# Routed feed-forward stage: blocks of two experts in turn, strips of 512 columns, whole 8 KB places

## The chip, the cores and the metric

The kernel runs on one core of a Trainium2 chip. The metric is device time in microseconds of one execution, with all weights read from HBM. The engines that matter are TensorE (PE, with its weight loads shown as PEld), VectorE (DVE), ScalarE (ACT), GpSimd (POOL) and SyncE (SP), which issues the weight transfers.

## What is computed

Two model blocks follow each other on 256 tokens of width 1024, in float32. The first block has two layers of token mixer and feed-forward; in its second layer the feed-forward is routed:

```python
logits = t @ router_w + router_b
top_v, top_i = lax.top_k(logits, 2)              # 2 of 8 experts for each token
gates = softmax(top_v)
combine = sum(one_hot(top_i, 8) * gates[..., None], axis=1)
for e in range(8):
    y_e = (silu(t @ w_gate[e]) * (t @ w_up[e])) @ w_down[e]   # 1024 -> 3584 -> 1024
    out = out + combine[:, e:e + 1] * y_e
```

The second block has two layers of feed-forward (2816 wide), latent attention with a convolution, and another feed-forward. Only the routed stage is rewritten by the change; elsewhere some buffers are allocated in other units.

## The kernel before

The stages run one after the other: `mix0, ffn0, mix1, moe, f1_0, mla0, f2_0, f1_1, mla1, f2_1`. The weights are laid out in HBM as units of 128 rows by 2048 float32 (1 MB, 8 KB in each partition), in the order in which they are used; `weight_plan` writes that order, and `Stream` loads unit after unit through SP's queue. A unit goes into a *place*. Four places (`RAW`) serve the whole program. In the routed stage more are lent: two from a pool of its own, six from the buffers of split weights (`hl`), and some from pools that lie idle then. `load()` issues the next transfer as soon as the queue of free places holds one. A transfer's issue on SP waits until the last reader of that place is done; `give` returns the places of a step at the step's end, and SP runs in program order.

In the routed stage (`moe`) each expert has 96 slots for tokens, in three groups of 32. `gather` brings the tokens of a pair of experts into `xe`. The work is cut into 56 steps, expert by expert, 7 blocks of 512 hidden columns each. A block takes four units for gate and up (woven: 128 columns of gate, 128 of up, and so on) and two for down.

- `gate_up` (L1076 to L1092): the 32 tokens of a group are the stationary operand, so that one matmul fills 32 of the 128 output partitions. Four matmuls that stand in four strips of the array run at once; each strip takes 256 columns of the unit. ACT takes SiLU of the gate half, DVE multiplies by the up half.
- `turn_g` (L1094 to L1102) transposes the product with matmuls of 32 columns against the identity.
- `down` (L1104 to L1128) multiplies by the down units, again 32 tokens stationary and four strips of 256 columns, and adds up in PSUM over the 7 blocks. After the last block the sums go to `yf`.
- `back` (L1130) splits `yf` in a high and a low part and scatters it to the tokens, scaled by the gate.

Groups 0 and 1 (`main`) are always computed, group 2 (`rest`) only when the expert has more than 64 tokens: its gate_up, turn and down stand in one `tc.If(counts[c] > 64)` at the end of the step (L1181). With 64 tokens or fewer every engine jumps over that code. In this text a *heavy* expert has more than 64 tokens and a *light* one has not. A second `If` (L1170), in step 15, holds the whole code for experts with more than 96 tokens (`second`); it does not run with these inputs. Before it every engine must still get past it. In step i the order on PE is gate_up of block i, down of block i-1, turn of block i, then the rest.

All fp32 matmuls that are not marked float32r show as two instructions in the trace, each with a weight load of its own.

Of the kernel before, what the change touches and what calls it, by code (L numbers as in the profile page):

```python
# [18 lines left out]
D = 1024  # L19
# [14 lines left out]
MORE = 2  # L34
STAGES = ("mix0", "ffn0", "mix1", "moe", "f1_0", "mla0", "f2_0", "f1_1", "mla1", "f2_1")


def blocks_of(f):
    return [(f0, min(512, f - f0)) for f0 in range(0, f, 512)]

# [30 lines left out]
def weight_plan(stages):  # L71
# [30 lines left out]
    def plan_moe():  # L102
        seq = [(e, b) for e in range(NE) for b in range(F1 // 512)]
# [162 lines left out]
def model(ctx, tc, A, out, stages=STAGES):  # L266
# [47 lines left out]
    turn = load_rows([("norm1_g", 16)], tp, "gl", nc.sync, 4)  # L314
# [95 lines left out]
    def xt():  # L410
        return [xp.tile([128, 8, 128], F32R, tag=n, name=n) for n in ("xh", "xl")]
# [89 lines left out]
    def ffn(key, f, nin, nout, half=None):  # L501
# [37 lines left out]
        def turn_g(b, tag="mm"):  # L539
            w = bl[b][1] // 128  # L540
            g = g32.pop(b)
            gh[b], gl[b] = [], []
            for t in range(2):
                ps = turn4([g[t][:, i * 128:(i + 1) * 128] for i in range(w)], tag)
                h = tp.tile([128, 4, 128], F32R, tag="gh", name="gh", bufs=4)
                l = tp.tile([128, 4, 128], F32R, tag="gl", name="gl", bufs=4)
                cut2(h[:, :w], l[:, :w], ps)
                gh[b].append(h)
                gl[b].append(l)
# [54 lines left out]
    def mixer1(l, nin, nout, c, pool):  # L604
# [27 lines left out]
        a_sb = []  # L632
        for t in range(2):
            a = tp.tile([128, 512], F32, tag="gl", name="az", bufs=4)
            nc.scalar.activation(a[:, :256], ps_a[t][:, :256], AF.Copy, scale=nin.r[t])
            a_sb.append(a)
        ps_g = project(("gx", l), 2, nin, 512, K2)
        z, zw = [], []
        for t in range(2):
            b = a_sb[t][:, 256:]  # L640
            nc.scalar.activation(b, ps_g[t][:, :256], AF.Copy, scale=nin.r[t])
            nc.vector.scalar_tensor_tensor(b, ps_g[t][:, 256:], nin.r[t], b, ALU.mult, ALU.mult)
            z.append(b)
            q = tp.tile([128, 2, 256], F32, tag="gl", name="zw", bufs=4)
# [15 lines left out]
        dT2 = tp.tile([128, 2, 256], F32, tag="gh", name="dT", bufs=4)  # L660
# [12 lines left out]
        for t in range(2):  # L673
            ac = tp.tile([128, 2, 256], F32, tag="gh", name="ac", bufs=4)
# [89 lines left out]
    def mla(l, nin, nout, c, pool):  # L764
# [68 lines left out]
        for nm, n, g in (("q", 3, "q_latent_norm_2"), ("k", 2, "kv_latent_norm_2")):  # L833
            for t in range(2):
                lh[nm, t], ll[nm, t] = (tp.tile([128, 4, 128], F32R, tag=i, name="lat", bufs=4)[:, :n] for i in ("gh", "gl"))
                cut2(lh[nm, t], ll[nm, t], turn4([lat[nm, t][0][:, i * 128:(i + 1) * 128] for i in range(n)]), gain(g, l))
# [95 lines left out]
        with tc.high_priority(offset=100):  # L932
            for t in range(2):
# [10 lines left out]
                s = tp.tile([128, 4, 128], F32, tag="gl", name="cs", bufs=4)  # L944
# [90 lines left out]
    def moe(R, nout, pool):  # L1035
# [3 lines left out]
        seq = [(e, b) for e in range(NE) for b in range(nb)]  # L1039
# [6 lines left out]
        def lent(p, names, w=D, **kw):  # L1046
            return lambda: [p.tile([128, w], F32, tag=n, name="raw", **kw) for n in names]
# [28 lines left out]

        def gate_up(i, gs):

            e, b = seq[i]
            if ("gu", i) not in held:  # L1080
                held["gu", i] = [W.hold(((("moe", e), "gu", b), j)) for j in range(4)]
            units = held["gu", i]
            ps, n = bank(), len(gs)
# [5 lines left out]
            s = prod[i, gs] = tp.tile([128, 512], F32, tag="g32", name="gs", bufs=4)[:, :n * 128].rearrange("p (g c) -> p g c", g=n)  # L1089
            v = ps[:, :n * 256].rearrange("p (g c) -> p g c", g=n)  # L1090
            nc.scalar.activation(s, v[:, :, 0:128], AF.Silu)  # L1091
            nc.vector.tensor_tensor(s, v[:, :, 128:256], s, op=ALU.mult)  # L1092

        def turn_g(i, gs):  # L1094

            s, n = prod.pop((i, gs)), len(gs)
            ps = bank()
            for g in range(n):
                for c in range(4):
                    nc.tensor.matmul(ps[32 * c:32 * c + 32, g * 128:(g + 1) * 128], s[:, g, 32 * c:32 * c + 32], ident, start=True, stop=True)  # L1100
            a = gT[i, gs] = pool.tile([128, n, 128], F32, tag=f"gT{gs[0]}", name="gT", bufs=2)
            nc.scalar.activation(a, ps[:, :n * 128].rearrange("p (g c) -> p g c", g=n), AF.Copy)  # L1102

        def down(i, gs):  # L1104
# [4 lines left out]
            for g in gs:  # L1109
                if b == 0:  # L1110
                    y[e, g] = bank("acc")
            a = gT.pop((i, gs))
            for j in range(4):
                for c, g in enumerate(gs):
                    for q in range(4):
                        nc.tensor.matmul(y[e, g][32 * q:32 * q + 32, :256], a[:, c, 32 * j:32 * j + 32], units[j // 2][0](j % 2, q * 256, 256),  # L1116
                                         start=b == 0 and j == 0, stop=b == nb - 1 and j == 3)
            if b == nb - 1:
                if e not in yf:
                    yf[e] = pool.tile([SLOTS, D], F32, tag="yf", name="yf", bufs=1)  # L1120
                    nc.gpsimd.memset(yf[e][64:SLOTS], 0.0)
                for g in gs:
                    for q in range(4):
                        o, a = yf[e][32 * g:32 * g + 32, q * 256:(q + 1) * 256], y[e, g][32 * q:32 * q + 32, :256]
                        if q % 2:
                            nc.vector.tensor_copy(o, a)
                        else:
                            nc.scalar.activation(o, a, AF.Copy)  # L1128
# [25 lines left out]
        for i in range(n + 1):  # L1154
            e, b = seq[i] if i < n else (NE, 0)
            now, before_ = [], []
            if i < n:
                gate_up(i, main)
                now += [lambda: gate_up(i, rest)]
            if i == 0:  # L1160
                _, counts = nc.values_load_multi_w_load_instructions(R.counts[0:1, :NE + 1], min_val=0, max_val=T,
                                                                            skip_runtime_bounds_check_because="the values are only compared")
# [6 lines left out]
            if (e, b) == (2, 1):  # L1169
                with tc.If(counts[NE] > SLOTS, preferred_fallthrough_block=False):  # L1170
                    for base in range(SLOTS, T, 128):
                        second(R, base)
            if i:
                down(i - 1, main)
                (now if b else before_).append(lambda: down(i - 1, rest))
            if i < n:
                turn_g(i, main)
                now += [lambda: turn_g(i, rest)]
            for c, fs in ((e - 1, before_), (e, now)):
                if fs:  # L1180
                    with tc.If(counts[c] > 64):  # L1181
                        for f in fs:
                            f()
            W.give(held.pop(("gu", i), []) + held.pop(("d", i - 1), []))
            if i and b == 0:
                back(e - 1)
# [81 lines left out]
    def post_of(ap):  # L1268
        t = xp.tile([128, D], F32, tag="xh", name="post")
# [69 lines left out]
```

## Time and profile before

| | |
|---|---|
| median of 3 runs | 2383.78 us (2382.59 to 2389.35) |
| the profiled execution's own time | 2385.31 us |
| its span, first to last instruction | 2382.9 us |
| mean granted TensorE clock | 0.976 |
| PE busy | 2253.9 us (95%) |
| DMA packets | 599.95 MB, mean 252 GB/s |

The span is what the profile covers; the execution's own time is 2.4 us longer. The time of a kernel on PE is not read from its busy share here: matmuls of one strip overlap with those of the others, so a stretch in which PE is busy can be one in which it waits a little after each instruction. What is read is the length of stretches, PE's idle time in them, and the granted clock.

### The profile page before, as it was taken

What the parts mean: (1) busy time and instruction counts of PE and PEld (TensorE: products, weight loads), DVE (VectorE), ACT (ScalarE), POOL (GpSimd) and SP (SyncE); (2) the same over time, 40 slices, a digit from 0 to 9 for tenths busy, and PEclk for the clock granted to TensorE, in tenths of its full rate; (3) what the DMA queues carried; (4) which work ended last, traced back from release to release, by engine and by line L of the source; (5) the groups of instructions that cost most, each with busy time, mean ns of one, the idle gap of its engine ahead of it and who ended that gap; (6) DMA issues with size and microseconds to landing.
All of it is one profiled execution on the core that took longest, in us unless ns stands there. A gap on an engine that the chain in (4) does not pass through costs nothing. (4 is left out here: it accounts for less than half of the span.)

```text
span 2382.9 us, 49084 instructions
## 1 busy us (share of the span) xinstructions
PE 2253.9 (95%) x21632; PEld 1746.0 (73%) x21632; DVE 929.2 (39%) x1262; ACT 795.0 (33%) x1259; POOL 171.2 (7%) x258
## 2 busy tenths in 40 slices
PE   8999999889989989988998899998999999989998
PEld 7888888556757656755675588886888888877887
DVE  5654564201010101010110354576645645587554
ACT  5544444101010101010110344465534544475443
POOL 3000012000000000000000100042000100050000
PEclk9999999899999999999999899999999999999999
DMA  7655554899979999999999655440555455432552
GB/s 270 222 190 185 187 210 179 323 379 402 366 289 403 382 406 390 399 392 396 382 395 389 224 210 182 167 177 21 201 180 190 177 189 182 148 130 94 198 179 87
DMA packets 112529, 599.95 MB, mean 252 GB/s; under 512 B 14652, under 2 KB 17118, under 8 KB 50204
## 3 DMA queue, kind: packets, MB, share of 16 engines
q1 hardware_dynamic: 111996, 595.82, 66.1%
q8 instruction: 195, 3.19, 0.5%
q10 hardware_dynamic: 288, 0.52, 0.1%
q14 instruction: 50, 0.41, 0.0%
HBM read 595.25 MB, written 1.05 MB: 250 GB/s over the span
## 5 line engine op out<-in xcount | busy, mean ns | idle before, releaser
L231 DVE TENSOR_TENSOR wl<-raw,wh 128x1024 fp32r<-128x1024 f32 (+2 forms) x456 | 540.7, 1216 | 430.9 <-ACT wh L230 430.5
L230 ACT ACTIVATE wh<-raw 128x1024 fp32r<-128x1024 f32 (+2 forms) x456 | 454.3, 1035 | 484.2 <-PE mm L391 302.3
L1087 PE MATMUL mm<-raw,xe 128*32 128x256 f32 x8960 | 535.9, 390 | 30.8 <-issue 26.9
L1087 PEld LDWEIGHTS mm<-raw,xe 128*32 128x32 f32 x8960 | 340.6, 113 | 192.8 <-issue 51.0
L388 PE MATMUL mm<-wh,xh 128*128 128x512 f32 (+3 forms) x1280 | 472.9, 372 | 3.1 <-ACT xh L407 3.1
L389 PE MATMUL mm<-wl,xh 128*128 128x512 f32 (+3 forms) x1280 | 471.3, 371 | 0.0
L391 PE MATMUL mm<-wh,xl 128*128 128x512 f32 (+3 forms) x1280 | 394.3, 371 | 0.3 <-DVE xl L408 0.3
L1092 DVE TENSOR_TENSOR gs<-mm,gs 128x256 f32<-128x256 f32 (+1 forms) x84 | 32.0, 380 | 741.5 <-ACT gs L1091 465.5
L1116 PE MATMUL acc<-raw,gT 128*32 128x256 f32 x4480 | 277.8, 386 | 16.4 <-PEq L1181 8.7
L388 PEld LDWEIGHTS mm<-wh,xh 128*128 128x128 f32 x1280 | 241.6, 189 | 44.0 <-ACT xh L407 3.5
L389 PEld LDWEIGHTS mm<-wl,xh 128*128 128x128 f32 x1280 | 241.8, 189 | 40.8 <-DVE wl L231 0.6
L391 PEld LDWEIGHTS mm<-wh,xl 128*128 128x128 f32 x1280 | 236.8, 189 | 41.0 <-DVE xl L408 1.0
L1116 PEld LDWEIGHTS acc<-raw,gT 128*32 128x32 f32 x4480 | 172.9, 112 | 97.3 <-issue 24.4
L1091 ACT ACTIVATE gs<-mm 128x256 f32<-128x256 f32 (+1 forms) x84 | 29.2, 348 | 598.9 <-PE mm L1087 598.9
L388 PE MATMUL acc<-wh,gh 128*128 128x512 f32 x464 | 186.0, 401 | 0.0
L389 PE MATMUL acc<-wl,gh 128*128 128x512 f32 x464 | 183.4, 395 | 0.0
L391 PE MATMUL acc<-wh,gl 128*128 128x512 f32 x464 | 145.3, 393 | 0.0
L371 POOL TENSOR_SCALAR s<-s 128x1 f32<-128x1 f32 (+1 forms) x60 | 32.3, 538 | 1171.2 <-ACT junk L378 1068.3
L391 PEld LDWEIGHTS acc<-wh,gl 128*128 128x128 f32 x464 | 87.3, 188 | 20.7
L389 PEld LDWEIGHTS acc<-wl,gh 128*128 128x128 f32 x464 | 87.6, 189 | 19.0
L388 PEld LDWEIGHTS acc<-wh,gh 128*128 128x128 f32 x464 | 87.5, 188 | 18.7
L1102 ACT ACTIVATE gT<-mm 128x256 f32<-128x256 f32 (+1 forms) x84 | 28.6, 348 | 186.4 <-PE mm L1100 186.1
(256 smaller groups left out, 1694.4 us busy)
## 6 DMA issues: line engine op xcount, KB each, us to landing
raw<-in_w_moe_dram SPq DMA_DIRECT2D x268, 1024.0 KB
raw<-in_w_f_dram SPq DMA_DIRECT2D x132, 1024.0 KB
raw<-in_w_moe_dram SPq DMA_DIRECT2D x184, 256.0 KB
raw<-in_w_ffn_dram SPq DMA_DIRECT2D x42, 1024.0 KB
raw<-in_w_mix_dram SPq DMA_DIRECT2D x23, 1024.0 KB
raw<-in_w_moe_dram SPq DMA_DIRECT2D x44, 512.0 KB
raw<-in_w_mla_dram SPq DMA_DIRECT2D x18, 1024.0 KB
raw<-in_w_mla_dram SPq DMA_DIRECT2D x8, 576.0 KB
```

The source lines that it names most:

```text
L230: self.nc.scalar.activation(h[:, s], t, AF.Copy)
L231: self.nc.vector.tensor_tensor(l[:, s], t, h[:, s].bitcast(F32), op=ALU.subtract)
L371: nc.gpsimd.tensor_scalar(r, ms, EPS, None, ALU.add)
L388: nc.tensor.matmul(o, sh[:, k, :], h[:, j, a:b], start=first and i == 0, stop=False)
L389: nc.tensor.matmul(o, sh[:, k, :], l[:, j, a:b], start=False, stop=False)
L391: nc.tensor.matmul(o, sl[:, k, :], h[:, i + (r[0] if r else 0), a:b], start=False, stop=last and i == n - 1)
L1087: nc.tensor.matmul(ps[32 * j:32 * j + 32, c * 256:(c + 1) * 256], xe[e // 2][:, k, e % 2, 32 * g:32 * g + 32], units[k // 2][0](k % 2, j * ...
L1091: nc.scalar.activation(s, v[:, :, 0:128], AF.Silu)
L1092: nc.vector.tensor_tensor(s, v[:, :, 128:256], s, op=ALU.mult)
L1102: nc.scalar.activation(a, ps[:, :n * 128].rearrange("p (g c) -> p g c", g=n), AF.Copy)
L1116: nc.tensor.matmul(y[e, g][32 * q:32 * q + 32, :256], a[:, c, 32 * j:32 * j + 32], units[j // 2][0](j % 2, q * 256, 256), start=b == 0 and ...
```

## The change

The order of the blocks comes from `moe_order`: block 0 of expert 0, block 0 of expert 1, block 1 of expert 0, and so on, pair by pair. The plan of the weights follows it. Down comes two steps after gate_up (`LAG = 2`), so that it belongs to the same expert as the block whose gate_up runs, except at the change of pairs. For two groups together the four strips are now (group 0, columns 0 to 511), (group 0, 512 to 1023), (group 1, ...), (group 1, ...): one matmul has 512 columns. The turn is one 128x128 transpose for each 128 columns. All places that are lent are now whole units: `xh` and `xl` are one tile `x`, and `gh` and `gl` of two token tiles are one tile `ghl` (the places out of `gn` and `t32` are gone). The `If` around `second` loses its argument on which side falls through.

```diff
+def moe_order():
+    return [(e, b) for p in range(0, NE, 2) for b in range(F1 // 512) for e in (p, p + 1)]
...
-            if i:
-                dn(*seq[i - 1])
-        dn(*seq[-1])
+            if i >= LAG:
+                dn(*seq[i - LAG])
+        for s in seq[-LAG:]:
+            dn(*s)
...
     def xt():
-        return [xp.tile([128, 8, 128], F32R, tag=n, name=n) for n in ("xh", "xl")]
+        x = xp.tile([128, 2, 8, 128], F32R, tag="x", name="xhl")
+        return [x[:, 0], x[:, 1]]
+
+    def quarters(dt, shape=(4, 128)):
+        a = tp.tile([128, 2, 2, *shape], dt, tag="ghl", name="ghl")
+        return [[a[:, i, t] for t in range(2)] for i in range(2)]
...
-        W.extend([(lent(hlp, (n,), UNIT), end - 6) for n in ("wh", "wl") * HL]
-                 + [(lent(xp, ("xh", "xl")), end - 16), (lent(xp, ("xh", "xl")), first + 30)]
-                 + [(lent(tp, ("gh", "gh", "gl", "gl"), 512, bufs=4), end - 16)] * 2
-                 + [(lent(tp, ("gn", "gn", "t32", "t32"), 512), first + 70)])
+        W.extend([(lent(hlp, n), end - 6) for n in ("wh", "wl") * HL] + [(lent(xp, "x"), end - 16), (lent(xp, "x"), first + 30 * LAG)]
+                 + [(lent(tp, "ghl"), end)] * 2)
...
+        def strips(gs):
+            return [(g, c) for g in gs for c in range(4 // len(gs))]
...
-            for c, g in enumerate(gs):
-                for k in range(8):
-                    for j in range(4):
-                        nc.tensor.matmul(ps[32 * j:32 * j + 32, c * 256:(c + 1) * 256], xe[e // 2][:, k, e % 2, 32 * g:32 * g + 32],
-                                         units[k // 2][0](k % 2, j * 256, 256), start=k == 0, stop=k == 7)
+            n = 256 * len(gs)
+            ps = bank()
+            for k in range(8):
+                for j, (g, c) in enumerate(strips(gs)):
+                    nc.tensor.matmul(ps[32 * j:32 * j + 32, :n], xe[e // 2][:, k, e % 2, 32 * g:32 * g + 32],
+                                     units[k // 2][0](k % 2, c * n, n), start=k == 0, stop=k == 7)
...
-            for g in range(n):
-                for c in range(4):
-                    nc.tensor.matmul(ps[32 * c:32 * c + 32, g * 128:(g + 1) * 128], s[:, g, 32 * c:32 * c + 32], ident, start=True, stop=True)
-            a = gT[i, gs] = pool.tile([128, n, 128], F32, tag=f"gT{gs[0]}", name="gT", bufs=2)
+            for q in range(n):
+                nc.tensor.transpose(ps[:, q * 128:(q + 1) * 128], s[:, q], ident)
+            a = gT[i, gs] = pool.tile([128, n, 128], F32, tag=f"gT{gs[0]}", name="gT", bufs=LAG + 1)
...
+            for k in range(4):
+                for j, (g, c) in enumerate(strips(gs)):
+                    at = (k // n + (g - gs[0]) * 2) * 32
+                    nc.tensor.matmul(o[32 * j:32 * j + 32, :w], a[:, k % n, at:at + 32], units[k // 2][0](k % 2, c * w, w),
+                                     start=b == 0 and k == 0, stop=b == nb - 1 and k == 3)
...
-            if (e, b) == (2, 1):
-                with tc.If(counts[NE] > SLOTS, preferred_fallthrough_block=False):
+            if i == 2 * nb + 1:
+                with tc.If(counts[NE] > SLOTS):
...
-            if i:
-                down(i - 1, main)
-                (now if b else before_).append(lambda: down(i - 1, rest))
+            if j >= 0:
+                down(j, main)
+                (now if i < n and seq[j][0] == e else late).append(lambda: down(j, rest))
```

The order of PE's instructions in one step in the middle of an expert, before. `xe` is the gathered tokens, `gT` the turned product, `gs` the product; what stands between the two kinds of branch runs for heavy experts only.

```order
L1087 MATMUL mm<-raw,xe 32x256 x64
L1116 MATMUL acc<-raw,gT 32x256 x32
L1100 MATMUL mm<-c_81,gs 32x128
L1181 COMPARE_AND_BRANCH
L1087 MATMUL mm<-raw,xe 32x256 x32
L1116 MATMUL acc<-raw,gT 32x256 x16
L1100 MATMUL mm<-c_81,gs 32x128 x4
L1181 UNCONDITIONAL_BRANCH x2
L1100 MATMUL mm<-c_81,gs 32x128 x7
```

The same place on PE in the changed kernel, one step in the middle of an expert.

```order
L1098 MATMUL mm<-raw,xe 32x512 x32
L1126 MATMUL acc<-raw,gT 32x512 x16
L1110 MATMUL mm<-c_81,gs 128x128
L1191 COMPARE_AND_BRANCH
L1098 MATMUL mm<-raw,xe 32x256 x32
L1126 MATMUL acc<-raw,gT 32x256 x16
L1110 MATMUL mm<-c_81,gs 128x128
L1191 UNCONDITIONAL_BRANCH x2
L1110 MATMUL mm<-c_81,gs 128x128
```

Before the branch the 64 and 32 matmuls have become 32 and 16 of twice the columns, the eight small turning matmuls two full transposes; the code that light experts jump over has lost three of its 52.

SP's queue, the first transfers of routed weights, before: places of two and of four pieces stand among the whole ones.

```order
L210 DMA raw<-in_w_moe_dram 128x2048 x12
L210 DMA raw<-in_w_moe_dram 128x1024 x4
L210 DMA raw<-in_w_moe_dram 128x512 x12
```

The same place in the changed kernel.

```order
L217 DMA raw<-in_w_moe_dram 128x2048 x16
```

Every transfer is now one of 128 runs of 8 KB; 17 places at the start have become 16.

## Rows read from the trace of the kernel before

**Rows 1.** The page's first line

```profile
span 2382.9 us, 49084 instructions
```

**Rows 2.** Transfers of routed weights: queue, count, size of one

```profile
raw<-in_w_moe_dram SPq DMA_DIRECT2D x268, 1024.0 KB
...
raw<-in_w_moe_dram SPq DMA_DIRECT2D x184, 256.0 KB
raw<-in_w_moe_dram SPq DMA_DIRECT2D x44, 512.0 KB
```

**Rows 3.** Stretches: length, busy of each engine (count), granted clock, DMA share, GB/s

```profile
440.00:450.00 10.00, 7.18 (x109) 4.26 (x105) 0.42 (x1) 0.77 (x2) 0.00 (x0) 0.83 0.23 78
443.00:543.00 100.00, 83.18 (x1411) 50.72 (x1407) 2.98 (x7) 5.50 (x15) 0.00 (x0) 0.91 0.92 360
543.00:663.00 120.00, 118.94 (x2199) 82.16 (x2191) 11.78 (x25) 12.85 (x37) 0.94 (x1) 1.00 0.97 382
663.00:791.00 128.00, 119.66 (x2205) 83.36 (x2198) 12.45 (x29) 12.96 (x37) 0.94 (x1) 0.96 0.87 344
791.00:899.00 108.00, 92.78 (x1537) 61.12 (x1530) 10.66 (x20) 9.85 (x25) 0.95 (x1) 0.95 1.01 404
899.00:1015.00 116.00, 114.88 (x2162) 79.23 (x2158) 11.80 (x27) 11.63 (x34) 0.94 (x1) 1.00 1.00 394
1015.00:1123.00 108.00, 92.31 (x1547) 61.33 (x1540) 10.66 (x20) 10.29 (x25) 0.94 (x1) 0.95 0.99 390
1123.00:1241.00 118.00, 115.72 (x2157) 80.19 (x2152) 10.74 (x23) 11.70 (x34) 0.94 (x1) 1.00 0.99 393
1241.00:1347.00 106.00, 89.78 (x1440) 58.23 (x1432) 9.36 (x18) 9.59 (x24) 0.94 (x1) 0.90 0.87 339
450.00:1331.00 881.00, 810.97 (x14402) 547.58 (x14397) 79.58 (x167) 82.29 (x220) 6.61 (x7) 0.97 0.96 380
```

**Rows 4.** PE's waits, 791 to 899 (expert 3): us, times, longest

```profile
PE mm L1087 <- issue: 8.6, 4, 4.0
PE mm L1100 <- PEq L1181: 3.8, 4, 2.1
PE mm L1070 <- issue: 1.2, 1, 1.2
```

**Rows 5.** PE's waits, 899 to 1015 (expert 4)

```profile
PE mm L1100 <- DVE gs L1092: 0.7, 1, 0.7
```

**Rows 6.** Queue of instruction blocks, 791 to 899: packets, MB, share

```profile
q8 instruction: 17, 0.28, 1.0%
```

**Rows 7.** Queue of instruction blocks, 899 to 1015

```profile
q8 instruction: 17, 0.28, 0.9%
```

**Rows 8.** Instructions in order, 1045 to 1068 (expert 5): start, length

```profile
1053.94 6.82 PE L1087 MATMUL mm<-raw,xe 128*32 128x256 f32 x89 [3.70 <-issue]
...
1066.84 0.53 PE L1100 MATMUL mm<-c,gs 128*32 128x128 f32 x11 [2.62 <-PEq L1181]
```

**Rows 9.** Instructions in order, 951 to 968 (expert 4)

```profile
950.71 0.42 DVE L1092 TENSOR_TENSOR gs<-mm,gs 128x256 f32<-128x256 f32 x1 [8.90 <-ACT gs L1091]
...
958.69 0.83 PE L1100 MATMUL mm<-c,gs 128*32 128x128 f32 x22
...
966.90 0.42 DVE L1092 TENSOR_TENSOR gs<-mm,gs 128x256 f32<-128x256 f32 x1 [8.90 <-ACT gs L1091]
```

**Rows 10.** DMA packets, 804 to 880: count by size, rate

```profile
DMA packets 6209, 31.03 MB, mean 408 GB/s; under 512 B 693, under 2 KB 693, under 8 KB 3184
```

**Rows 11.** DMA packets, 1052 to 1062

```profile
DMA packets 575, 4.19 MB, mean 419 GB/s; under 512 B 65, under 2 KB 65, under 8 KB 65
```

**Rows 12.** After the second If, 676 to 706, in order

```profile
690.97 5.89 PE L1116 MATMUL acc<-raw,gT 128*32 128x256 f32 x64 [7.09 <-DMA raw<-in_w_moe_dram]
```

**Rows 13.** From strips of 32 to full width and back, 1249 to 1259

```profile
1250.30 0.53 PEld L1145 LDWEIGHTS mm<-xh,ST 96*128 96x128 f32 x3 [0.41 <-issue]
1250.30 0.97 PE L1145 MATMUL mm<-xh,ST 96*128 96x512 f32 x3
...
1251.20 4.52 PE L1087 MATMUL mm<-raw,xe 128*32 128x256 f32 x80
```

**Rows 14.** Last down of the stage, 1344 to 1348

```profile
1345.28 1.93 PE L1116 MATMUL acc<-raw,gT 128*32 128x256 f32 x32 [0.19 <-PEq L1181]
```

More of the change, by code (lines that the diff above doesn't have):

```diff
@@ L102, in plan_moe @@
     def plan_moe():
-        seq = [(e, b) for e in range(NE) for b in range(F1 // 512)]
+        seq = moe_order()
         def dn(e, b):
@@ L643, in mixer1 @@
             z.append(b)
[L644 removed]
+            q = qs[t].rearrange("p (k c) -> p k c", k=2)
             for k in range(2):
@@ L673, in mixer1 @@
         for t in range(2):
-            ac = tp.tile([128, 2, 256], F32, tag="gh", name="ac", bufs=4)
+            ac = acs[t]
             b = ac[:, 1]
@@ L1038, in moe @@
         nb = F1 // 512
-        seq = [(e, b) for e in range(NE) for b in range(nb)]
+        seq = moe_order()
         xe, S, y, yf, gT, prod, held = {}, {}, {}, {}, {}, {}, {}
@@ L1108, in down @@
             units = held["d", i]
[L1109 to L1117, printed above, removed]
+            n, w = len(gs), 256 * len(gs)
+            if b == 0:
+                y[e, gs] = bank("acc")
+            a, o = gT.pop((i, gs)), y[e, gs]
+            for k in range(4):
[3 more added lines that the diff above has]
+                                     start=b == 0 and k == 0, stop=b == nb - 1 and k == 3)
             if b == nb - 1:
@@ L1121, in down @@
                     nc.gpsimd.memset(yf[e][64:SLOTS], 0.0)
[L1122 to L1128, printed above, removed]
+                for j, (g, c) in enumerate(strips(gs)):
+                    r, v = yf[e][32 * g:32 * g + 32, c * w:(c + 1) * w], o[32 * j:32 * j + 32, :w]
+                    if j % 2:
+                        nc.vector.tensor_copy(r, v)
+                    else:
+                        nc.scalar.activation(r, v, AF.Copy)
         def back(e):
@@ L1153, in moe @@
         gather(0)
-        for i in range(n + 1):
-            e, b = seq[i] if i < n else (NE, 0)
-            now, before_ = [], []
+        for i in range(n + LAG):
+            j = i - LAG
+            now, late = [], []
             if i < n:
+                e, b = seq[i]
                 gate_up(i, main)
-                now += [lambda: gate_up(i, rest)]
+                now.append(lambda: gate_up(i, rest))
             if i == 0:
                 _, counts = nc.values_load_multi_w_load_instructions(R.counts[0:1, :NE + 1], min_val=0, max_val=T,
-                                                                            skip_runtime_bounds_check_because="the values are only compared")
+                                                                     skip_runtime_bounds_check_because="the values are only compared")
             if i == 2:
@@ L1168, in moe @@
                 todo.popleft()()
-            if (e, b) == (2, 1):
-                with tc.If(counts[NE] > SLOTS, preferred_fallthrough_block=False):
+            if i == 2 * nb + 1:
+                with tc.If(counts[NE] > SLOTS):
                     for base in range(SLOTS, T, 128):
                         second(R, base)
-            if i:
-                down(i - 1, main)
-                (now if b else before_).append(lambda: down(i - 1, rest))
+            if j >= 0:
+                down(j, main)
+                (now if i < n and seq[j][0] == e else late).append(lambda: down(j, rest))
             if i < n:
                 turn_g(i, main)
-                now += [lambda: turn_g(i, rest)]
-            for c, fs in ((e - 1, before_), (e, now)):
+                now.append(lambda: turn_g(i, rest))
+            for at, fs in ((j, late), (i, now)):
                 if fs:
-                    with tc.If(counts[c] > 64):
+                    with tc.If(counts[seq[at][0]] > 64):
                         for f in fs:
                             f()
-            W.give(held.pop(("gu", i), []) + held.pop(("d", i - 1), []))
-            if i and b == 0:
-                back(e - 1)
+            W.give(held.pop(("gu", i), []) + held.pop(("d", j), []))
+            if j >= 0 and seq[j][1] == nb - 1:
+                back(seq[j][0])
             if i < n and e % 2 == 1 and b == nb - 3 and e < NE - 1:
```

41 lines of the change are left out of this document (19 added, 22 removed).

## The prediction, made before the changed kernel ran

> **What bounds the kernel now.** I read the page first (span 2382.9 us [rows 1]), then the transfers of the routed stage, then the stage in stretches of one expert, then PE's waits in a stretch of each kind, then the instructions of single steps.
>
> The stage moves 268 + 184/4 + 44/2 = 336 units of 1 MB [rows 2], 352 MB. Its stretches [rows 3] start where the first gate_up of an expert ends; the stage runs from 443 to the last down, which starts at 1345.28 and ends near 1347 [rows 14]: 904 us. The windows show two kinds of expert. Experts 1, 2, 4 and 6 carry some 2160 to 2205 PE matmuls and the clock is granted in full, except for one place in expert 2: these are heavy. Experts 0, 3, 5 and 7 carry 1411 to 1547: light. Heavy steps are bound by PE: from one product on DVE to the next it takes 966.90 - 950.71 = 16.19 us [rows 9], and PE waits for nothing over 0.7 us [rows 5]. The surprise is in the light experts. A light step has two thirds of the work, about 16.2 x 2/3 = 10.8 us, and takes 108/7 = 15.4 us. That is not for want of weights: PE's waits there name no transfer of any weight, but "issue" and the sequencer at the branch, 8.6 + 3.8 + 1.2 = 13.6 us in one expert [rows 4], with stops of 3.70 us in the midst of straight code and 2.62 us behind the branch [rows 8]. "Issue" means that no instruction was there.
>
> The queue of instruction blocks tells why. A heavy expert executes 2162 + 2158 = 4320 PE instructions and 17 blocks arrive [rows 3, 7]: 254 to a block. A light one executes 1537 + 1530 = 3067, and 17 blocks arrive as well [rows 3, 6]: the code that is jumped over is fetched too. It is 52 matmuls a step, each two instructions with two loads, so 7 x 208 = 1456, and (3067 + 1456)/17 = 266. So a block lasts 116/17 = 6.8 us in a heavy expert without a stop, and 108/17 = 6.4 us in a light one, with stops: I read 6.4 us as the fastest that blocks come while the weight queue is full.
>
> DMA is the second bound, close behind: shares of 0.99 to 1.01 at 390 to 404 GB/s in the stretches from 791 on, but 0.87 and 0.92 in others [rows 3].
>
> What PE needs is its busy time less what the low clock cost. [...] Over the eight stretches busy is 827, the loss 9 + 0 + 5 + 5.4 + 0 + 5.4 + 0 + 10.6 = 35, so the need is 792 us of 904. Idle are 77. The four light experts lose 16.8 + 15.2 + 15.7 + 16.2 = 64 idle and 30 by the clock, 94 together, 3.4 us a step.
>
> **The change part by part.**
> *Strips of 512 columns.* The columns streamed stay the same: half the matmuls, each twice as long. That saves PE nothing. It halves the instructions before the branch: 64 + 32 + 8 matmuls become 32 + 16 + 2, that is 416 instructions become about 196; the skipped code stays near 194. A step is then 390 instructions instead of 624, 1.5 blocks instead of 2.4. A light step of 11 us needs a block each 7.2 us, slower than the 6.4 at which they come. What remains: a block that holds all of the skipped code lasts only 61 x 11/196 = 3.4 us, and PE stops for the other 3.0. The code lies so in a quarter of positions and half so in about as many; averaged over positions that is some 1.1 us a light step against the 3.4 of now. I keep a quarter to a third of the 94: 24 us. Both ends: 0 (no stop is left) and 94 (the stop belongs to the jump, not to the amount of code).
>
> [...]
>
> *Turns as full transposes.* PE leaves the strips for the full width and comes back: 2 crossings in a light step, 4 in a heavy one, 168 in all. [...] 168 x 0.13 = 22 us. The turns themselves shrink: 22 of the small matmuls take about 0.83 us now [rows 9], about 0.6 a heavy step and 0.4 a light one, of which half goes: 13 us. Net I take +11 us; ends -13 (crossing free) and 168 x 0.41 - 13 = +56.
>
> [...]
>
> *Alternating blocks.* The pairs are (0, 1), (2, 3), (4, 5), (6, 7): by rows 3 each has one light and one heavy expert. That the change does not mix is thereby excluded. A pair of steps needs 16.2 + 11 us of PE against 12 units, 12.6 MB, of DMA. At 410 GB/s these are 30.7 us. So PE no longer falls behind for seven steps at a time, the places are no longer all full, and DMA need not pause. Down two steps later moves each down and its two units to the step of the next block of the same expert; nothing new is waited for, since the turned product has a buffer more.
>
> *Whole places.* With short packets about (3184 of 6209 are under 8 KB) the rate is 408 GB/s [rows 10]; in a stretch where only 65 semaphore packets are short it is 419 [rows 11]. From 450 to 1331 the stage moved 881 x 380 GB/s = 335 MB [rows 3]. At 419 that takes 799 us.
>
> *The second If.* Before step 16 PE stands 7.09 us and then runs 64 matmuls in 5.89 us at the low clock, where 64 x 4.52/80 = 3.6 would do [rows 12, 13]. Both versions jump over the same code. I leave the whole 12 us (7 idle, 5 clock in that stretch); with places not full DMA goes on meanwhile. Ends: 0 and 24, if the other layout costs one more fetch.
>
> *The end.* Two experts finish in neighbouring steps with one buffer `yf`: the second's copies wait until the first is split, and the first cut of the next stage's weights waits behind them on ACT. I put 4 us on the path, ends 0 and 10. Tiles `x` and `ghl` in the other stages hold the same bytes and the order of instructions there is the same: 0, ends -2 and +3.
>
> **Sum.** PE path: 792 + 11 + 24 + 12 = 839 us, so the last down ends at 443 + 839 = 1282. DMA path: 450 + 799 + 10 for pauses (before, 4% of 881 = 35; the pause at 440 to 450, share 0.23 [rows 3], lies ahead of the 450 and stays) = 1259, and 16 from there to the last down as now (1331 to 1347): 1275. Two limits within 7 us of each other, with ten units between them (16 places less the six of a step), do not reach either: I add 12, and 4 for the end. 1282 + 16 = 1298 against 1347: 49 us less. The profiled execution took 2385.31, 1.5 above the median of the runs; 2385 - 49 = 2336.
>
> **Rivals.**
> *The stops stay by half.* 803 + 47 + 12 = 862, plus 443, 12 and 4: 1321, 26 us less, 2359. For it: the branch itself shows 2.62 us [rows 8]. Against it: four of the stops, 8.6 us, lie in code without a branch [rows 4].
> *The stops go wholly and DMA alone decides.* 1275 + 4 = 1279: 68 less, 2317. For it: heavy experts at 6.8 us a block show none. Against it: the skipped code shortens some blocks.
> *Slower: the stop belongs to the jump.* Each light step keeps its 3.4 us: 803 + 94 + 12 + 4 = 913 against 904, so 9 more, 2394. It decides from the point where more than 85 of the 94 us stay, 3.0 us for each of the 28 jumps. For it: 28 jumps before and after, over almost the same code. Against it: the same row of waits, and that both kinds of expert fetch 17 blocks.
>
> **How the numbers follow.** Forecast 0.55, stops by half 0.22, DMA alone 0.15, slower 0.08. A measurement of this kernel tells apart about 0.3%, 7 us. The forecast and the DMA case are faster; of the half case a fifth, where nearly all stays, is no change. Faster 0.88, same 0.05, slower 0.07. The likeliest's own range is 2318 to 2354 (crossing and If priced at their nearer ends); the whole range reaches to 2308 for the DMA rate with no pause and to 2370 for two thirds of the stops.
>
> **What would show it.** Light steps of 11 to 13 us where PE does not wait for weights, and waits on weight transfers (named by `raw`) instead of "issue"; about 10 instruction blocks for each seven steps instead of 17; no routed packets of 2 or 4 KB and 410 to 419 GB/s; a stage of about 855 us. Wrong: "issue" and branch waits still near 14 us per light expert (the rival of the jump); heavy steps over 16.8 us (crossings dearer than 0.13); DMA share below 0.95 with PE waiting (places given back too late); or any other stage changed by more than 3 us.

## The result and the profile after

The changed kernel takes 2351.51 us (median of 4 runs, 2345.89 to 2354.2), the kernel before, on the same chip, 2386.36. The ratio is 0.9852, with a 95% interval from 0.9826 to 0.9877: 35 us less. The profiled execution took 2354.2 us.

The first line of the page of the changed kernel, and its row of routed transfers, answer to [rows 1, 2]: a quarter of the instructions is gone, and all 336 units come whole.

```profile
span 2352.4 us, 36128 instructions
...
raw<-in_w_moe_dram SPq DMA_DIRECT2D x336, 1024.0 KB
```

The stretches of the changed kernel, with the columns of [rows 3] (length, busy time of PE, PEld, DVE, ACT, POOL with counts, granted clock, DMA share, GB/s). An expert no longer has a stretch of its own, so the first row stands for the whole stage, the second for the part in which the transfers run, and the last for all that comes behind the stage.

```profile
443.00:1310.00 867.00, 806.66 (x8324) 300.78 (x8316) 78.20 (x155) 82.06 (x210) 6.61 (x7) 0.99 0.95 392
450.00:1294.00 844.00, 789.36 (x8196) 294.57 (x8188) 71.42 (x145) 77.93 (x202) 5.67 (x6) 0.99 0.98 403
1310.00:2352.00 1042.00, 1007.30 (x4884) 840.00 (x4876) 604.07 (x777) 511.65 (x756) 105.39 (x172) 0.98 0.45 159
```

The last downs of the stage answer to [rows 14]: they end near 1312, where before it was 1347. So the stage is 869 us long instead of 904.

```profile
1308.01 4.08 PE L1126 MATMUL acc<-raw,gT 128*32 128x512 f32 x22
```

PE's waits in the changed kernel from 450 to 1290 (us, times, longest) answer to [rows 4, 5].

```profile
PE mm L1110 <- DVE gs L1103: 20.1, 22, 1.0
PE mm L1110 <- DVEq L1191: 17.3, 18, 1.0
PE mm L1110 <- DVEq L1180: 5.1, 1, 5.1
PE acc L1126 <- PEq L1191: 3.0, 15, 0.5
...
PE mm L1110 <- PEq L1191: 2.0, 1, 2.0
PE mm L1098 <- issue: 1.7, 2, 1.3
```

This is the view to read. "Issue" and the branch, 13.6 us in one light expert before, are down to 1.7 + 3.0 us from 450 to 1290, nearly the whole stage. Waits for transfers of weights come to 0.2 us in the whole view, so the waits on `raw` that the prediction named as its sign did not come. In their place the turn (L1110) waits 37.4 us for the product that DVE makes, in 40 stops of at most 1.0 us. Four of these (2.9 us) stand behind the gate_up of group 2, and the kernel before has the same four; the other 36 are new. The reader is to see that the second row names DVE's sequencer at the branch and means the same wait: the stop that ends at 950.17 (below) carries that name, and the product of 949.69 + 0.43 ends just ahead of it.

The kernel before, in the same view from 450 to 1290, has five rows of "issue" and the branch that add to 45.0 us. The two largest:

```profile
PE mm L1087 <- issue: 22.4, 9, 4.0
PE mm L1100 <- PEq L1181: 16.9, 17, 2.8
```

The instruction blocks from 450 to 1290 (packets, MB, share), first in the changed kernel, then in the kernel before:

```profile
q8 instruction: 86, 1.41, 0.7%
```

```profile
q8 instruction: 130, 2.13, 1.0%
```

Where each stop sits is shown by PE's instructions in order, 944 to 992 in the changed kernel, which answer to [rows 8, 9]: start, length, tile sizes, count, idle time before.

```profile
950.17 0.44 PE L1110 MATMUL mm<-c,gs 128*128 128x128 f32 x2 [0.97 <-DVEq L1191]
950.54 1.93 PE L1126 MATMUL acc<-raw,gT 128*32 128x512 f32 x16
952.64 1.92 PE L1126 MATMUL acc<-raw,gT 128*32 128x512 f32 x16 [0.18 <-PEq L1191]
954.35 7.08 PE L1098 MATMUL mm<-raw,xe 128*32 128x512 f32 x64
962.39 0.44 PE L1110 MATMUL mm<-c,gs 128*128 128x128 f32 x2 [0.95 <-DVE gs L1103]
962.75 1.92 PE L1126 MATMUL acc<-raw,gT 128*32 128x512 f32 x16
```

Gate_up ends, the turn comes at once and PE stands until the product is there; only then comes the down, cut in two halves, one before the branch and one behind it. Before, the down lay between gate_up and turn and covered ACT and DVE [rows 9]. The program still says down and then turn; the scheduler put the whole turn ahead of the down in 32 of the 56 steps, and its first half in four more. The order quoted ahead of the prediction is one of the steps in which it did not.

The products of the changed kernel give the step: 961.90 - 949.69 = 12.2 us for a light one, 979.32 - 961.90 = 17.4 for a heavy one, 29.6 a pair.

```profile
949.69 0.43 DVE L1103 TENSOR_TENSOR gs<-mm,gs 128x256 f32<-128x256 f32 x1 [10.52 <-ACT gs L1102]
961.90 0.42 DVE L1103 TENSOR_TENSOR gs<-mm,gs 128x256 f32<-128x256 f32 x1 [11.79 <-ACT gs L1102]
...
979.32 0.42 DVE L1103 TENSOR_TENSOR gs<-mm,gs 128x256 f32<-128x256 f32 x1 [10.52 <-ACT gs L1102]
```

The packets of the changed kernel from 800 to 830 answer to [rows 10, 11]: nothing of 2 or 4 KB among them.

```profile
DMA packets 1731, 12.62 MB, mean 421 GB/s; under 512 B 193, under 2 KB 193, under 8 KB 193
```

### The profile page after: what moved, and what is told of

It is laid out like the page before. It is cut to its first block, busy times and chain, and to the rows that moved or that the text cites. A ratio compares the mean times of both kernels' runs of the same rounds, so it can differ in the third digit from the quotient of the medians.

```text
span 2352.4 us, 36128 instructions
## 1 busy us (share of the span) xinstructions
PE 2241.6 (95%) x15276; PEld 1493.8 (63%) x15276; DVE 926.4 (39%) x1246; ACT 794.2 (34%) x1243; POOL 166.5 (7%) x258
## 5 line engine op out<-in xcount | busy, mean ns | idle before, releaser
L237 ACT ACTIVATE wh<-raw 128x1024 fp32r<-128x1024 f32 (+2 forms) x456 | 454.7, 1036 | 484.8 <-PE mm L398 301.7
L1098 PE MATMUL mm<-raw,xe 128*32 128x512 f32 (+1 forms) x5376 | 506.6, 525 | 1.9 <-issue 1.7
L395 PE MATMUL mm<-wh,xhl 128*128 128x512 f32 (+3 forms) x1280 | 473.1, 372 | 2.6 <-ACT xhl L414 2.6
L396 PE MATMUL mm<-wl,xhl 128*128 128x512 f32 (+3 forms) x1280 | 471.2, 370 | 0.0
L398 PE MATMUL mm<-wh,xhl 128*128 128x512 f32 (+3 forms) x1280 | 394.0, 371 | 0.0
L1098 PEld LDWEIGHTS mm<-raw,xe 128*32 128x32 f32 x5376 | 180.5, 110 | 300.4 <-issue 257.3
L1126 PE MATMUL acc<-raw,gT 128*32 128x512 f32 (+1 forms) x2688 | 270.6, 526 | 3.6 <-PEq L1191 3.2
L395 PEld LDWEIGHTS mm<-wh,xhl 128*128 128x128 f32 x1280 | 241.6, 189 | 43.5 <-ACT xhl L414 3.0
L396 PEld LDWEIGHTS mm<-wl,xhl 128*128 128x128 f32 x1280 | 241.5, 189 | 40.8 <-DVE wl L238 0.6
L398 PEld LDWEIGHTS mm<-wh,xhl 128*128 128x128 f32 x1280 | 236.7, 189 | 40.8 <-DVE xhl L415 0.7
L395 PE MATMUL acc<-wh,ghl 128*128 128x512 f32 x464 | 186.0, 401 | 0.0
L396 PE MATMUL acc<-wl,ghl 128*128 128x512 f32 x464 | 183.4, 395 | 0.0
L1126 PEld LDWEIGHTS acc<-raw,gT 128*32 128x32 f32 x2688 | 83.4, 110 | 134.3 <-issue 109.6
L398 PE MATMUL acc<-wh,ghl 128*128 128x512 f32 x464 | 145.3, 393 | 0.0
L398 PEld LDWEIGHTS acc<-wh,ghl 128*128 128x128 f32 x464 | 87.3, 188 | 20.8
L395 PEld LDWEIGHTS acc<-wh,ghl 128*128 128x128 f32 x464 | 87.5, 188 | 18.7
L1110 PEld LDWEIGHTS mm<-c,gs 128*128 128x128 f32 x140 | 16.5, 140 | 110.0 <-DVE gs L1103 42.7
```

The lines of the kernel that those rows point to most:

```text
L237: self.nc.scalar.activation(h[:, s], t, AF.Copy)
L395: nc.tensor.matmul(o, sh[:, k, :], h[:, j, a:b], start=first and i == 0, stop=False)
L396: nc.tensor.matmul(o, sh[:, k, :], l[:, j, a:b], start=False, stop=False)
L398: nc.tensor.matmul(o, sl[:, k, :], h[:, i + (r[0] if r else 0), a:b], start=False, stop=last and i == n - 1)
L1098: nc.tensor.matmul(ps[32 * j:32 * j + 32, :n], xe[e // 2][:, k, e % 2, 32 * g:32 * g + 32], units[k // 2][0](k % 2, c * n, n), start=k == ...
L1126: nc.tensor.matmul(o[32 * j:32 * j + 32, :w], a[:, k % n, at:at + 32], units[k // 2][0](k % 2, c * w, w), start=b == 0 and k == 0, stop=b ...
```

## The experiments

Theory: PE's path bounds the changed kernel, and the turn's new place on PE is the part of it that the prediction missed. Rival: the transfers bound it already.

### Turns queued behind the whole down

```diff
+                m = nc.tensor.matmul(...)          # in down; its last one is returned
...
-                down(j, main)
+                behind = tc.issue_after(down(j, main))
...
-                turn_g(i, main)
+                with behind:
+                    turn_g(i, main)
```

> The changed kernel with one edit: the two turning transposes of a step are queued on PE behind the whole down of that step. In the changed kernel the scheduler put them straight behind gate_up, and PE stands some 0.95 us there in each of the 56 steps until ACT and DVE have made the product. Theory A (PE is the bound of the routed stage, and these stops are the part of its path that the prediction missed): the stops vanish, 53 us less of PE; then the weight transfers decide (450 + 799 us at 419 GB/s + some pauses + 16 from the last landing to the last down), so the stage ends near 1280 instead of 1310 and the time is 20 to 32 us below the changed kernel's 2352, near 2325. DMA pauses (bins with a share under 0.95 between 460 and the last landing) shrink from about 30 us to under 15. Rival B (the transfers are the bound already, PE's stops are covered by them): the time stays within 7 us of 2352, and PE waits on raw instead.

Measured: 2324.32 us, ratio to the kernel before 0.9766 (0.9748 to 0.9784). That is 27 us below the changed kernel by the medians, 21 by the two ratios. The theory holds. PE's waits from 450 to 1290 in this run:

```profile
PE acc L1126 <- DMA raw<-in_w_moe_dram: 9.9, 7, 5.4
PE mm L1110 <- DVEq L1181: 8.1, 1, 8.1
...
PE mm L1110 <- DVE gs L1103: 2.9, 4, 0.7
```

The waits for the product are 2.9 us instead of 37.4, and weights appear. The 56 stops and 53 us of the expectation were too many: 36 stops with 34.5 us went. PE's instructions of a light step in this run, and the stretches of stage and rest:

```profile
953.52 7.08 PE L1098 MATMUL mm<-raw,xe 128*32 128x512 f32 x64
960.41 3.62 PE L1126 MATMUL acc<-raw,gT 128*32 128x512 f32 x32
963.96 0.78 PE L1110 MATMUL mm<-c,gs 128*128 128x128 f32 x2
964.66 7.07 PE L1098 MATMUL mm<-raw,xe 128*32 128x512 f32 x64
```

```profile
450.00:1268.00 818.00, 786.98 (x8204) 290.54 (x8200) 71.98 (x146) 76.87 (x205) 5.67 (x6) 0.99 1.00 411
1283.00:2319.00 1036.00, 1000.10 (x4868) 835.95 (x4868) 603.82 (x776) 510.11 (x754) 107.36 (x172) 0.98 0.45 159
```

A light step is 964.66 - 953.52 = 11.1 us, without a stop. PE lost 34.5 us of stops, the kernel 27 us: from 450 to 1268 the DMA share is 1.00, with one pause of 5 to 6 us near 650 (313 GB/s from 639 to 660), so the transfers are the bound now, and PE gives a part back in waits on weights (9.9 us in the first row). This is the fastest of the kernels that compute everything.

### Strips of 256 columns

```diff
-                    nc.tensor.matmul(ps[32*j:32*j+32, :n], ..., units[k // 2][0](k % 2, c * n, n), ...)
+                    h = n if k == 0 else 256
+                    for x in range(0, n, h):
+                        nc.tensor.matmul(ps[32*j:32*j+32, x:x+h], ..., units[k // 2][0](k % 2, c * n + x, h), ...)
```

The down is cut alike. Both runs have the alternating order; the second also has the turns behind the whole down.

> The changed kernel with strips of 256 columns again (nearly every 512-column matmul of gate_up and down for two groups is split in two), same order of blocks, same whole places, same full transposes, same place of the turns. Columns streamed are the same; PE instructions a step go back from about 390 to about 600. Theory A (code volume and the rate at which instruction blocks arrive cause the stops): 4.8 blocks a pair of steps at 6.4 us are 31 us against 29.6 of PE work, and the light step, 2.4 blocks in 12.2 us, stops for about 3 us: waits put down to issue and to the branch return with 2 to 3.4 us a light step, the stage is 40 to 90 us longer, the time 2390 to 2440. Rival B (the alternation of light and heavy steps alone cured the stops, since blocks are fetched ahead during the heavy step): under 12 us longer, 2352 to 2364. Rival C (the stop belongs to the jump): no change, and no stops, since there are none now.

Measured: 2381.12 us, ratio 0.9994 (0.9982 to 1.0006). All of the gain is gone (30 us by the medians, 34 by the ratios). The number lies between the ranges of theory A and rival B, so neither is right in size. Stops of theory A's kind are back, but "issue" and the branch come to 19 us from 450 to 1290, where the theory has 2 to 3.4 us a light step; rows from 450 to 1290:

```profile
PE mm L1112 <- DVE gs L1105: 18.8, 21, 0.9
PE mm L1112 <- DVEq L1195: 16.0, 17, 1.0
PE mm L1100 <- issue: 7.3, 6, 1.6
...
PE acc L1130 <- PEq L1195: 5.1, 15, 1.1
PE acc L1130 <- issue: 4.5, 2, 2.6
```

The waits for the product stay (34.8 us), so this run does not give back the kernel before: it loses the same time in other places. Part of the 30 us is not stops at all: a heavy step, with a wait of 0.94 us for the product, takes 17.56 us here and 17.42 in the changed kernel.

> Alternating order, whole places, turns queued behind the whole down, but strips of 256 columns, so PE executes about 600 instructions a step. With the turns ahead the same kernel took 2381, its waits on issue and on the branch came to some 20 us in the stage, against 54 in the kernel before, and 35 us went to PE standing for the product. Theory A (the stops come of code volume, but the alternation lets the heavy step's time serve the light step's fetching, so most of them are gone in either order of turns): the 35 us and more come back, 2335 to 2350. Rival B (blocks come at 6.4 us at best, 4.8 a pair make 31 us whatever PE does, and time freed elsewhere turns into waits on issue): 2362 to 2381.

Measured: 2347.65 us, ratio 0.9852 (0.9833 to 0.9871): theory A. The same columns in half the instructions are worth 2347.65 - 2324.32 = 23 us here. Of the freed time a part turned into stops all the same (rows of this run, 450 to 1290):

```profile
PE mm L1100 <- issue: 14.4, 12, 1.6
PE mm L1112 <- PEq L1198: 9.5, 9, 2.6
```

Not all of the 23 us is stops. From gate_up to gate_up, a light step without a stop takes 557.92 - 546.65 = 11.27 us here and 11.14 in the run of 2324 us; a heavy one, from product to product, takes 16.51 here and 961.07 - 944.69 = 16.38 there. That is 0.13 us a step, some 7 us in 56 steps. The two products of the run of 2324 us:

```profile
944.69 0.42 DVE L1103 TENSOR_TENSOR gs<-mm,gs 128x256 f32<-128x256 f32 x1 [10.72 <-ACT gs L1102]
...
961.07 0.42 DVE L1103 TENSOR_TENSOR gs<-mm,gs 128x256 f32<-128x256 f32 x1 [8.91 <-ACTq L1194]
```

### The old order

```diff
-LAG = 2
+LAG = 1
-    return [(e, b) for p in range(0, NE, 2) for b in range(F1 // 512) for e in (p, p + 1)]
+    return [(e, b) for e in range(NE) for b in range(F1 // 512)]
```

Three runs: on the changed kernel, with the turns behind the whole down, and with that and strips of 256.

> The changed kernel with the old order: expert by expert, down one step after gate_up; strips of 512, full transposes and whole places stay. The scheduler puts the turns straight behind gate_up here too, so PE's step is the same (12.2 light, 17.4 heavy). Theory A (places hold some ten units ahead, 25 us of DMA, enough to carry a light expert: 85 us of PE against 105 - 25 of transfers; the alternation is worth little): within 15 us of the changed kernel, 2340 to 2367. Rival B (the alternation is what pays: a light expert runs at the transfers' pace, 15.1 us a step, a heavy one at PE's 17.4): 28 pairs at 32.5 instead of 30 us, 40 to 70 us longer, 2390 to 2420, with PE waits on raw in the light experts.

Measured: 2342.68 us, ratio 0.9831 (0.9812 to 0.9851), where the changed kernel has 0.9852 (0.9826 to 0.9877). The intervals overlap: with strips of 512 the alternation gained nothing, theory A.

> The old order (expert by expert, down one step later) together with the turns queued behind the whole down; strips of 512, full transposes, whole places. The alternating kernel with the turns behind took 2324 us. A pair of steps needs 27.5 us of PE there (11.1 + 16.4) and 30.1 of transfers. Theory A (transfers are the bound now and some ten units are held ahead, so the order of the blocks is worth nothing): 2317 to 2331. Rival B (a light expert, 78 us of PE against 105 of transfers with 25 in hand, waits for weights, and a heavy one, 115 us of PE, fills the places so that transfers pause): PE waits on raw in experts 3, 5 and 7, DMA pauses in 2, 4 and 6, and the time is 8 to 25 us longer, 2332 to 2350.

Measured: 2325.54 us, ratio 0.9761 (0.9743 to 0.9779), against 2324.32. Theory A in time; but rival B's rows are there too, small. PE's waits from 450 to 1290 in this run:

```profile
PE mm L1098 <- DMA raw<-in_w_moe_dram: 9.8, 18, 1.1
PE acc L1126 <- DMA raw<-in_w_moe_dram: 9.4, 14, 2.2
```

They are 19 us of PE, and the time does not show them; I take it that PE has them to spare, as in the run of 2324 us.

> Strips of 256, old order (expert by expert, down one step later), turns queued behind the whole down: of the change only the whole places and the full transposes are left. With alternating blocks the same kernel took 2348, the kernel before 2384. Theory A (in the code of 256-column strips the alternation is what lessens the stops, since a heavy step's time serves the light step's fetching): the stops of the light experts come back, 13 us an expert by the waits on issue and the branch, and the time is 2375 to 2390. Rival B (whole places gave the 36 us): 2345 to 2356, with few waits on issue.

Measured: 2363.32 us, ratio 0.9918 (0.9892 to 0.9945), between the ranges of the two theories: with strips of 256 the alternation is worth 16 us, but the other 20 us against the kernel before are neither's. The stops of this run, 450 to 1290:

```profile
PE mm L1112 <- PEq L1198: 16.9, 11, 3.3
PE mm L1100 <- issue: 15.7, 12, 2.6
```

With alternation the two rows add to 23.9 us, without it to 32.6, although the quicker kernel gets through more work in these 840 us.

### Pieces, and the old turns

The first edit fills four places in 2 or 4 transfers again (on the changed kernel, then on the run of 2363 us); the second turns by matmuls of 32 columns in the run of 2363 us.

```diff
+            q = c // getattr(place, 'pieces', 1)
+            parts = [(o[:, s:s + q], a[:, s:s + q]) for o, a in parts for s in range(0, c, q)]
```

```diff
-                nc.tensor.transpose(ps[:, q * 128:(q + 1) * 128], s[:, q], ident)
+                for c in range(4):
+                    nc.tensor.matmul(ps[32*c:32*c+32, q*128:(q+1)*128], s[:, q, 32*c:32*c+32], ident, start=True, stop=True)
```

> The changed kernel with the old packet sizes: the two places in x are filled in two transfers each, the two in ghl in four each, so a good part of the packets are 2 and 4 KB again; everything else stays. Theory A (PE is the bound in the stage): the rate while full falls from 419 to some 408 to 414 GB/s, which lengthens the transfers' own path by 8 to 20 us, but pauses shrink by as much; the time moves by 0 to 8 us. Rival B (transfers are the bound): 12 to 22 us longer, 2364 to 2374.

Measured: 2350.04 us, ratio 0.986 (0.984 to 0.988): theory A. Short packets were there, and the rate was lower (this run, 800 to 830), but PE did not wait for them (0.2 us on `raw` from 450 to 1290):

```profile
DMA packets 2677, 12.17 MB, mean 406 GB/s; under 512 B 298, under 2 KB 298, under 8 KB 1578
```

> Strips of 256, old order, turns behind the whole down, full transposes, as in the run of 2363 us, but with four of the places filled in 2 or 4 pieces again: of the change only the full transposes are left. Theory A (whole places gave the 20 us against the kernel before, by a quicker weight queue or by quicker instruction blocks): 2374 to 2386. Rival B (the full transposes gave it: 24 PE instructions fewer before the branch and 12 fewer behind it in a step, so fewer stops): 2358 to 2370.

Measured: 2361.08 us, ratio 0.9902 (0.988 to 0.9924): rival B, the same as with whole places.

> Strips of 256, old order, turns behind the whole down, whole places, as in the run of 2363 us, but the product is turned by matmuls of 32 columns as in the kernel before: of the change only the whole places are left, PE executes some 620 instructions a heavy step again. Theory A (whole places gave the 20 us): 2358 to 2368. Rival B (the full transposes gave it, by fewer instructions): 2374 to 2388, with waits on issue and the branch back at 45 us in the stage instead of 33.

Measured: 2374.21 us, ratio 0.9955 (0.9941 to 0.9969): rival B, at the lower end of its range. The full transposes are worth 11 us against the run of 2363 us and 13 against that of 2361. The waits from 450 to 1290:

```profile
PE mm L1113 <- PEq L1199: 20.3, 20, 4.9
PE mm L1100 <- issue: 19.4, 10, 3.9
PE mm L1113 <- issue: 5.3, 2, 4.2
```

45.0 us, where the run with full transposes had 32.6. The gain is one of fewer instructions and not of less work: by the two kernels a step has 28 PE instructions fewer before the branch and 14 fewer behind it (the expectation says 24 and 12), while PE's own work in a heavy step without a stop grows by the transposes. The products of such a step in the run with matmuls of 32 columns give 646.58 - 630.39 = 16.19 us, as in the kernel before [rows 9], and in the run of 2363 us, with full transposes, 605.08 - 588.57 = 16.51:

```profile
630.39 0.42 DVE L1105 TENSOR_TENSOR gs<-mm,gs 128x256 f32<-128x256 f32 x1 [6.98 <-ACT gs L1104]
...
646.58 0.42 DVE L1105 TENSOR_TENSOR gs<-mm,gs 128x256 f32<-128x256 f32 x1 [8.93 <-ACT gs L1104]
```

```profile
588.57 0.42 DVE L1105 TENSOR_TENSOR gs<-mm,gs 128x256 f32<-128x256 f32 x1 [9.00 <-ACT gs L1104]
...
605.08 0.42 DVE L1105 TENSOR_TENSOR gs<-mm,gs 128x256 f32<-128x256 f32 x1 [9.00 <-ACT gs L1104]
```

The 10 us from the run of 2374 us to the kernel before were not tried apart. The kernel before waits 7.1 and 2.9 us for weights in two places, of which one is [rows 12]; they are not among these rows, so how many places are lent, and when, is a candidate and no more.

### The second If

```diff
-                with tc.If(counts[NE] > SLOTS):
-                    for base in range(SLOTS, T, 128):
-                        second(R, base)
+                pass
```

> The alternating kernel with the turns behind the whole down (2324 us), with the second If left out: the code for experts with more than 96 tokens is not in the program. With it, PE stands 8.1 us for DVE at that place, its clock is low for 10.2 us right behind, and transfers pause for some 6 us at 645 to 655. Theory A (the price of the jump is PE's stop, and PE is not the bound, so only the pause of the transfers is gained): 4 to 9 us shorter, 2315 to 2320. Rival B (the whole stop and the low clock stand on the path): 11 to 15 us shorter, 2309 to 2313. Rival C (covered wholly): within 3 us.

Measured: 2317.04 us, ratio 0.9727 (0.971 to 0.9743): 7 us, theory A.

> The alternating kernel with the turns behind the whole down (2324 us), with the second If laid out as in the kernel before (preferred_fallthrough_block=False). Without that If the time was 2317. Theory A (with this layout the code that does not run stands out of the way, the jump goes the other way round): PE's stop of 8.1 us shrinks and up to 6 of the 7 us are gained, 2317 to 2321. Rival B (the layouts cost alike): 2322 to 2327.

Measured: 2327.9 us, ratio 0.9772 (0.9742 to 0.9801): no gain, rival B within a microsecond. PE's stop has other names and is no shorter, 12.0 us where the run of 2324 us has 8.1 + 1.1 (this run, 640 to 700):

```profile
PE mm L1110 <- issue: 6.7, 1, 6.7
PE mm L1110 <- PEq L1194: 5.3, 1, 5.3
```

## Why the prediction came out as it did

The sign and the range were right, and so was the main cause, the stops: 35 us less, where 49 were forecast and the whole range went from 2308 to 2370. That the time came so near is in part luck, since a wait that the sum did not have and stops that it kept too many of partly cancel. The rival of half the stops names 2359, nearer to 2351.5 than the forecast's 2336, but the 47 us of stops that it is made of are not there. Point by point:

*Code volume.* Right in kind. PE's waits on "issue" and the branch from 450 to 1290 are down from 45.0 us to 4.7, and the granted clock of the stage is up from 0.97 [rows 3] to 0.99, with 86 instruction blocks in place of 130. "Issue" by itself says only that the engine waited for nothing that the profile shows; that instructions were missing is borne out by two edits that each add code: matmuls of 32 columns for the turns (stops 32.6 to 45.0 us), and strips of 256 (4.7 to 19 us with the turns ahead). It is the amount of code and not the jump: the 28 light steps still jump, and the returns cost 3.0 us in all (L1126 <- PEq L1191). The rival of the jump is refuted. The 24 us kept for remaining stops were too many: 4.7 remain (3.0 + 1.7). The dear jump is another one, that over the whole code of `second`, where the branch and what hung on it held PE 5.1 + 2.0 us.

*Strips of 512.* "That saves PE nothing" does not hold: a step without a stop is 0.13 us shorter than with strips of 256, 7 us in all.

*Turns as full transposes.* This is the step that failed. It priced the crossings (+11 net) and not the place of the turn: it took for granted that PE would meet the turn behind the whole down, as before, and the scheduler put it ahead in 32 steps. That is a term of 37 us that no part of the sum had, 34.5 of it new. The sign named for dear crossings did fire, a heavy step over 16.8 us (17.4), but with the wrong reason beside it: with the turns behind the down a heavy step takes 16.4 us. No run shows the 0.13 us that the sum takes for one crossing; in the trace of the kernel before, matmuls of 512 float32r columns follow each other every 0.227 us (59.78 to 65.67), by which the three of [rows 13], 1251.20 - 1250.30 = 0.90 us, are 0.22 over, 0.11 for each crossing. What crossings and turns cost together is shown by the runs that differ in the turns alone: 16.51 - 16.19 = 0.32 us a heavy step. A light step without its stop takes 11.0 us in the kernel before (872.70 - 860.36, less a stop of 1.30; not the estimated 10.8) and 11.27 with strips of 256 and full transposes, 0.27 more. Each 28 times, these are 16 us, where 11 were priced (the prediction's own 22 - 13 is 9). At the 0.41 us of the weight-load row [rows 13] for each crossing the sum would have been 45 us longer; these 16 do not bear that price out.

*The sum again.* Forecast were 839 + 16 for the interplay and the end = 855. With 37 more for the product's waits, 5 more for the turns, 7 less for the strips and 19 less for the stops it is 871; the stage took 869, so some 14 of the 16 were used, and what they are stays open. The two large errors, 37 too little and 19 too much, partly cancel. The 35 us that the sum takes off PE's busy time for the low clock no run shows as such. What the traces show in the kernel before is a granted clock of 0.50 from 692.10 to 693.10 and of 1.00 from 697 to 698, and one stretch that can be compared: from 690.97 to 696.86 it was 0.61, and 0.61 x 5.89 = 3.6 us, what the 64 matmuls there take at 1.00 by [rows 13].

*Alternating blocks.* Forecast as what keeps PE and DMA in step. It isn't needed once the code is short: 2343 and 2326 without, 2352 and 2324 with it. With long code it is worth 16 us. The two edits cure the same stops, and their gains don't add: strips of 512 are worth 38 us without the alternation (2363 to 2326) and 23 with it (2348 to 2324). Read in one order, the runs with the turns behind the down lead from 2384 us (before) over 2374 (whole places and what else was not tried apart), 2363 (full transposes) and 2348 (alternation) to 2324 (strips of 512).

*Whole places.* The rate rose as forecast, to 419 and over, and was worth nothing here (2350 with pieces), since PE was the bound. On the kernel that the transfers bound (2324 us) pieces were not tried. The rival of DMA alone (2317) describes the kernel with the turns behind the down better, 2324 with DMA full to 1268; the path's end was forecast at 1259.

*The second If.* 12 us were kept, and leaving it out gained 7 in a kernel that DMA bounds. In the changed kernel it was not tried.

*Other stages.* Behind the stage the profile shows 4 to 5 us more than before: 2352.4 - 1312 = 1040, where it was 2382.9 - 1347 = 1036. The prediction named more than 3 us as a sign of being wrong. With the turns behind the down it is 1036 again. It is one profile of each, and its cause stays open.

## What to carry to other kernels

Where a scheduler may reorder, look at the whole order of the changed kernel for each instruction that waits for another engine, and count the steps that differ; one step is not a sample. Stops of 1 us are easily read over in a list that once had 4 us in it, and 40 of them were the largest item here. Two edits that shorten the same wait are to be priced as one, and what a faster engine gains is cut off at the next bound: here 34 us on PE became 27, or 21 by the ratios.

## What was not expected of the hardware

A third fewer instruction blocks (86 for 130) took nearly all of the stops away (45.0 us to 4.7), with the same jumps. The blocks are not simply late on average: with strips of 256 and the alternating order, 125 packets of the same queue came from 450 to 1290, about as many as the 120 of the old order, yet issue and branch held PE 24 us instead of 33. I take it that the light steps stop less when a heavy step, in which more time passes for each block (6.8 us against 6.4 in the kernel before, from [rows 3, 6, 7]), stands between them; no run tries that apart.

The lower rate with short packets cost nothing where it was tried: 406 GB/s with pieces and 421 without (800 to 830), and the same time in both pairs of runs (2350 and 2352, 2361 and 2363).
